# Two blocks side by side at the joints, and token-half sums out of PSUM

## The chip, the cores and the metric

The kernel runs on one core of one Trainium2 chip. The metric is device microseconds of a whole execution; before the change the median of three runs is 968.72 us (968.68 to 970.75). Engine names are those of the profile: PE is TensorE, PEld its weight loads, DVE is VectorE, ACT is ScalarE, POOL is GpSimd, and SP issues the large loads.

## The reference

One layer of a streaming encoder, with 512 tokens and 1024 features, all in float32:

```python
h = h + 0.5 * _swiglu(_rmsnorm(h, ffn1_norm[i]), ffn1_w_in[i], ffn1_w_out[i])
z = _rmsnorm(h, mix_norm[i]) @ w_in[i]
...
h = h + jnp.concatenate([y_conv, y_gla], axis=-1) @ w_out[i]
h = h + 0.5 * _swiglu(_rmsnorm(h, ffn2_norm[i]), ffn2_w_in[i], ffn2_w_out[i])
gate = jax.nn.sigmoid(_rmsnorm(h, ple_norm[i]) @ ple_w_gate[i])
h = h + gate * (p[i] @ ple_w_proj[i])
return _rmsnorm(h, final_norm)
```

What matters here is that four times a new norm of h feeds a projection. The norm's row factor is applied after the projection, so the projection itself takes h times the gain vector, transposed so that features lie on partitions.

## The kernel before, in words

Every float32 product is made of three fast matmuls. Each operand x is split into a high part H (x rounded to the fast format, a copy by ACT) and a low part L (x − H, by DVE), and a product is wH·xH, wH·xL and wL·xH, added up in PSUM (`mm3`, line 209). The program has seven PSUM banks for such sums (`bank`, line 96) and one more for small things (`aux`).

A **joint** is the place where one stage has finished h and the next one needs it transposed. There are three: from FFN1 to the mixer (around 365 us in the trace), from the mixer to FFN2 (around 546 us) and from FFN2 to the last stage, the embedding gate (around 895 us). `Turn` (line 427) does it: `half(e)` takes four of the eight feature chunks; `chunk(c)` transposes chunk c of the four token blocks into one bank by four PE transposes, splits it by `gsplit` (H on ACT, hgH in the trace; L on DVE, hgL; both read the bank and multiply by the gain), and, if the next stage wants it, calls `keep`. `half(0)` runs before the last piece of h is finished, `half(1)` after it. `rows` makes the row factors from the sums of squares, through DVE, a power on POOL and DVE again, and `spread` turns them by four transposes on PE.

`keep` (line 321) is for the two stages that multiply by a Strassen-like scheme with seven products of half size: FFN2 and the last stage (FFN1 keeps its own way and isn't touched). They need sums and differences of the token halves of h (tokens 0 to 255 and 256 to 511) and of its feature halves. `keep` makes two raw copies of a chunk, one per token half, by ACT from PSUM to SBUF, each 128 x 256 (xg in the trace). For FFN2 the sums follow from these raw copies: `sums1` (one subtraction of 128 x 512 per pair of chunks, on the early features) and `sums2` (three). `steps` lists the four calls with `operands`, and they are hung between the matmul blocks. The last stage has `row_sums` (line 1477), which adds two raw copies and subtracts the result from a third, and later `row_diff` and `row_last`.

At the joint itself TensorE runs two blocks over the eight chunks. In the mixer they are pb0 and pa0 (`zblock`, lines 938 to 955), in FFN2 g0 and u0 (`plain_block`, lines 1426 to 1434). First both blocks take the four early chunks, then `half(1)` transposes the four late ones, and then one block takes its late chunks and after it the other.

The order of work on PE, DVE and ACT is written by hand up to line 1658: `Ordered` chains each instruction behind the one before it on its engine as in the program text. From `in_order(False)` on, where the last stage's first product `times(x_, a11, b11, first=True)` and its `half(1)` stand, the planner chooses the order, within the data's dependences. POOL's and SP's order is the planner's throughout, nearly. Two engines that read one bank take turns: in the trace `keep`'s copies wait for hgL of the same chunk.

Of the kernel before, what the change touches and what calls it, by code (L numbers as in the profile page):

```python
# [15 lines left out]
P = 128  # L16
# [46 lines left out]
def block_kernel(ctx: ExitStack, tc: tile.TileContext, a: dict, out: bass.AP):  # L63
# [23 lines left out]
    def bt(dt=F32, s="a"):  # L87
        return big.tile([P, SEQ], dt, tag="A", bufs=NA, name=nm(s))
# [7 lines left out]
    def bank():  # L96
        return pp.tile([P, SEQ], F32, tag="mm", bufs=7, name=nm("ps"))
# [36 lines left out]
    def vec(name, c):  # L134
        return vcols[name, c]
# [27 lines left out]
    def gsplit(src, g, s):  # L163
        hi = bt(F32R, s + "H")
        act.activation(hi, src, AF.Copy, scale=g)
        lo = bt(F32R, s + "L")
        dve.scalar_tensor_tensor(out=lo, in0=src, scalar=g, in1=hi.bitcast(F32),
                                 op0=ALU.mult, op1=ALU.subtract)
        return hi, lo
# [63 lines left out]
    def zblock(w, x, mid={}, ps=None, ks=range(DC)):  # L233

        ps = ps if ps is not None else bank()
        for k in ks:
            if k in mid:
                mid[k]()
            wh, wl = rows_of(w, k)
            mm3(ps, wh, wl, *x[k], k == 0, k == DC - 1)  # L240
        return ps
# [57 lines left out]
    def two(t):  # L299
        return t.rearrange("p (k c) -> p k c", k=2)  # L300

    def sub(out, x, y):
        dve.tensor_tensor(out=out, in0=x, in1=y, op=ALU.subtract)
# [3 lines left out]
    class Right:  # L307
# [13 lines left out]
        def keep(self, ps, c, by_dve=False):  # L321

            k, jp, jj = c // 4, c % 4 // 2, c % 2
            for half in range(2):
# [5 lines left out]
                else:  # L330
                    act.activation(o, src, AF.Copy, scale=g)

        def sums1(self, jp):
            b11, b12 = self.raw[0, 0, jp], self.raw[0, 1, jp]
            sub(b11, b12, b11)
# [91 lines left out]
    class Turn:  # L427
# [6 lines left out]
        def done(self, t, e):  # L434
            act.activation(tmp("sq", bufs=3), h_of(t, e), AF.Square, accum_out=self.ss[:, e * TB + t:e * TB + t + 1])

        def chunk(self, c):
            ps = bank()
            for t in range(TB):
                pe.transpose(ps[:, t * P:(t + 1) * P], hall[:, t, c * P:(c + 1) * P], ident)  # L440
            self.hg.append(gsplit(ps, vec(self.gname, c), "hg"))
            if self.x is not None:
                self.x.keep(ps, c)

        def half(self, e):
            for c in range(4 * e, 4 * e + 4):
                self.chunk(c)

        def rows(self):
            ss = tmp("cs", 16)[:, :TB]  # L450
# [484 lines left out]
    low(w2b[1])  # L935
    w2a = [high(raw_a[0])]
    mid = []
    pb0 = zblock(wb[0], hg, ks=range(4))
    pa0 = zblock(wa[0], hg, ks=range(4))
    nxt.half(1)  # L940
    zblock(wb[0], hg, ps=pb0, ks=range(4, DC))
    gw = bt(s="gw")[:, 0:2 * DC * RANK].rearrange("p (k c) -> p k c", k=DC)
    pool.memset(gw, 0.0)
    nc.sync.dma_start(out=gw[:, :, 0:RANK], in_=w_in[:, C_G:C_G + RANK].rearrange("(k p) c -> p k c", p=P))
    w2a.append(high(raw_a[1]))
    raw_q = pair(C_Q)
    low(w2a[0])
    zblock(wa[0], hg, {4: lambda: mid.append(nxt.rows())}, pa0, range(4, DC))
    low(w2a[1])
    pb1 = zblock(wb[1], hg, {1: lambda: mid.append(spread(mid[0]))})  # L950
    rs, rsb = mid
# [472 lines left out]
        return ps  # L1424

    mid = []
    steps = xb.steps()
    g0 = plain_block(w0, 0, 0, ks=range(4))
    u0 = plain_block(w0, 1, 0, ks=range(4))
    nxt.half(1)  # L1430
    steps[0]()
    plain_block(w0, 0, 0, ps=g0, ks=range(4, DC))
    steps[1]()
    plain_block(w0, 1, 0, ps=u0, ks=range(4, DC))
    w1.fetch("a21", "a22")
    w1.add_part("a11", "a12")
    g1_ = plain_block(w0, 0, 1, {3: lambda: mid.append(nxt.rows()), 7: lambda: mid.append(spread(mid[0]))})
# [1 line left out]
    w2.fetch("a11", "a21", "a22", "a12")  # L1439
    w1.add_part("a21", "a22")  # L1440
    u1_ = plain_block(w0, 1, 1)
    steps[2]()
    steps[3]()
    hooks = sums_hooks(xb, ("t2", "t3", "t1", "t4"), (("h0", 1), ("h1", 1), ("h3", 1), ("m1", 2)))
    hooks.update({("h2", 1): lambda *_: w2.s12(), ("h4", 1): lambda *_: w2.s3_(), ("m7", 10): lambda *_: turn_p(0), ("m5", 10): lambda *_: turn_p(1)})

# [27 lines left out]

    HS = [slice(h * HALF, (h + 1) * HALF) for h in range(2)]

    def row_sums(jp):

        a11_, a21_, a22_ = (xp.raw[k, h, jp] for k, h in ((0, 0), (0, 1), (1, 1)))
        s1.append(a22_)  # L1480
        dve.tensor_tensor(out=a22_, in0=a21_, in1=a22_, op=ALU.add)
        n2.append(two(bt(s="n2")))
        sub(n2[jp], a11_, a22_)

    def q_high(to, src, jp):
        to.append(added(high(src[jp])))
# [24 lines left out]
                  ("d20", 1): todo((q_high, b21, q21, 1), (first_sum, 1), (third_sum, 1)),  # L1511
                  ("d20", 2): todo((final_in,))})
    hg = []
    xp = Right(hg, "ple_norm")
    nxt = Turn("ple_norm", xp)
    nxt.hg = hg
    rs2_ = mid
# [260 lines left out]
```

## Time and profile before

| | us |
|---|---|
| median of 3 runs | 968.72 |
| the profiled execution | 969.31 |
| its span | 967.5 |
| PE busy in the span | 948.2 |
| DVE busy | 722.5 |
| ACT busy | 476.5 |
| POOL busy | 56.2 |

The span reaches from the first to the last instruction; the execution's own time has 1.8 us around it. Numbers ahead of a row of the order of time are the start in us from the span's beginning, then the row's length; "x4" merges four neighbours alike, and the bracket at the end tells how long the engine had been idle and what ended that. A row of the stages gives for each engine its busy time and, in brackets, its instructions, and behind POOL the clock granted to TensorE as a share of full speed.

### The profile page before, as it was taken

How to read it: one execution, taken by the hardware profiler on the slowest of the kernel's cores; microseconds unless marked ns; L12 is line 12 of the kernel's file. 1: busy time of each engine (PE TensorE's matmuls, PEld its weight loads, DVE VectorE, ACT ScalarE, POOL GpSimd, SP SyncE). 2: the span in 40 equal slices, each digit the busy share in tenths (PEclk: the TensorE clock that was granted, in tenths of full speed). 3: DMA queues.
4: the chain of work that ended last, by engine and by line, in shares of the span. 5: the costliest groups of instructions: out<-in, count | busy, mean ns of one | idle time of the engine just before them, and what ended most of it. 6: DMA issues, size and time to landing. Idle time of an engine off the chain costs nothing.

```text
span 967.5 us, 14435 instructions
## 1 busy us (share of the span) xinstructions
PE 948.2 (98%) x5810; PEld 833.0 (86%) x5810; DVE 722.5 (75%) x967; ACT 476.5 (49%) x733; POOL 56.2 (6%) x71
## 2 busy tenths in 40 slices
PE   9999999999999999999999999999999999999895
PEld 7888999999999987788878689999999999998574
DVE  6775877877777567999985367777777768766796
ACT  5552444434443464473656564344433444345983
POOL 0000200000000111001210010000000000001121
PEclk9999999999999999999999999999999999999998
DMA  7541333243233594253563371432233322455452
GB/s 226 176 152 44 97 103 107 67 130 110 91 103 112 153 221 92 63 142 97 146 159 101 75 174 44 131 110 88 92 106 112 120 95 66 153 196 131 87 98 98
DMA packets 90214, 112.88 MB, mean 117 GB/s; under 512 B 5075, under 2 KB 65669, under 8 KB 90148
## 3 DMA queue, kind: packets, MB, share of 16 engines
q1 hardware_dynamic: 84260, 94.67, 31.1%
q0 software_dynamic: 5872, 17.30, 9.8%
q8 instruction: 45, 0.74, 0.3%
q14 instruction: 21, 0.17, 0.1%
q10 hardware_dynamic: 16, 0.00, 0.0%
HBM read 93.61 MB, written 2.10 MB: 99 GB/s over the span
## 4 chain that ended last, share of the span: by engine, by line
PE 93%; ACT 3%; DVE 2%; issue 0%; DMA 0%; POOL 0%; POOLq 0%; SPq 0%; ACTq 0%; DVEq 0%
PE ps L46 92%; ACT xg L46 1%; PE ax L46 1%; ACT hgH L46 1%; ACT wh L46 1%; ACT sq L46 1%; DMA wr<-in_ffn_w_in 0%; DVE hgL L46 0%; DVE g L46 0%; DVE s L46 0%; ACT wl L46 0%; DVE rs L46 0%; DVE y L46 0%; DVE sq L46 0%; DVE xg L46 0%
## 5 line engine op out<-in xcount | busy, mean ns | idle before, releaser
L46 PE MATMUL ps<-hgH,wh 128*128 128x256 f32 (+1 forms) x768 | 239.7, 317 | 2.2 <-ACT hgH L46 1.7
L46 PE MATMUL ps<-hgL,wh 128*128 128x256 f32 (+1 forms) x768 | 239.1, 316 | 0.3 <-DVE hgL L46 0.3
L46 PE MATMUL ps<-hgH,wl 128*128 128x256 f32 (+1 forms) x768 | 238.2, 315 | 0.0
L46 DVE TENSOR_TENSOR wl<-wr,wh 128x1024 fp32r<-128x1024 f32 (+1 forms) x158 | 188.6, 1208 | 61.0 <-ACT wh L46 60.8
L46 ACT CAST wh<-wr 128x1024 fp32r<-128x1024 f32 (+1 forms) x172 | 176.3, 1039 | 74.3 <-PE ps L46 41.4
L46 PEld LDWEIGHTS ps<-hgH,wh 128*128 128x128 f32 x768 | 146.9, 191 | 14.7 <-ACT hgH L46 4.3
L46 PEld LDWEIGHTS ps<-hgL,wh 128*128 128x128 f32 x768 | 146.6, 191 | 11.2 <-DVE hgL L46 1.9
L46 PEld LDWEIGHTS ps<-hgH,wl 128*128 128x128 f32 x768 | 147.0, 191 | 8.7
L46 PE MATMUL ps<-wh,actH 128*128 128x512 f32 x352 | 137.6, 391 | 0.0
L46 PE MATMUL ps<-wh,actL 128*128 128x512 f32 x352 | 137.3, 390 | 0.0
L46 PE MATMUL ps<-wl,actH 128*128 128x512 f32 x352 | 137.0, 389 | 0.0
L46 ACT ACTIVATE s<-g 128x512 f32<-128x512 f32 x48 | 30.4, 632 | 156.3 <-DVE g L46 156.3
L46 DVE SCALAR_TENSOR_TENSOR hall<-ps,rsh,hall 128x512 f32<-128x512 f32 x96 | 71.1, 747 | 30.1 <-PE ps L46 29.2
L46 DVE SCALAR_TENSOR_TENSOR cv<-glu,cw,cv 128x502 f32<-128x502 f32 (+24 forms) x120 | 81.0, 730 | 0.6
L46 PEld LDWEIGHTS ps<-wl,actH 128*128 128x128 f32 x352 | 66.1, 188 | 13.9
L46 PEld LDWEIGHTS ps<-wh,actH 128*128 128x128 f32 x352 | 66.2, 188 | 12.9
L46 PEld LDWEIGHTS ps<-wh,actL 128*128 128x128 f32 x352 | 66.2, 188 | 12.4
L46 ACT CAST wh<-sm 128x1024 fp32r<-128x1024 f32 x38 | 39.7, 1046 | 42.0 <-DVE sm L46 36.2
L46 DVE TENSOR_TENSOR wl<-sm,wh 128x1024 fp32r<-128x1024 f32 x38 | 46.3, 1220 | 4.6 <-ACT wh L46 4.3
L46 ACT COPY sq<-ps 128x512 f32<-128x512 f32 x38 | 22.1, 585 | 54.8 <-PE ps L46 54.8
L46 DVE SCALAR_TENSOR_TENSOR hgL<-ps,vcol,hgH 128x512 fp32r<-128x512 f32 x32 | 23.2, 748 | 30.9 <-ACT hgH L46 30.7
L46 DVE TENSOR_TENSOR sm<-wr,wr 128x1024 f32<-128x1024 f32 x17 | 21.0, 1236 | 29.5 <-DMA wr<-in_ffn_w_in 29.5
(247 smaller groups left out, 1691.7 us busy)
## 6 DMA issues: line engine op xcount, KB each, us to landing
wr<-in_ffn_w_in SPq DMA_DIRECT2D x84, 512.0 KB
wr<-in_ffn_w_out SPq DMA_DIRECT2D x44, 512.0 KB
wr<-in_w_in SPq DMA_DIRECT2D x20, 512.0 KB
wl<-wr POOLq DMA_DIRECT2D x15, 512.0 KB, 5.3
wr<-in_w_out SPq DMA_DIRECT2D x8, 512.0 KB
wq<-in_ple_w_gate SPq DMA_DIRECT2D x8, 512.0 KB
wl<-wq POOLq DMA_DIRECT2D x8, 512.0 KB, 4.6
wa<-wr POOLq DMA_DIRECT2D x12, 256.0 KB, 6.1
```

Source lines behind the costliest of these rows:

```text
L46: inst = call(*args, **kwargs)
```

## The change

It has three parts.

**The loop over k.** In the mixer and in FFN2 the two blocks at the joint run chunk by chunk: for each k first the one block's three matmuls, then the other's. `half(1)` stands ahead of k = 4, in the mixer `rows` ahead of k = 6 (it stood at the second block's fourth chunk, behind the memset and load of gw and one weight remainder).

**The four chunks first.** `half` makes all four chunks' transposes and splits, and only then whatever `turned` of the next stage gave back for each chunk.

**The sums from PSUM.** For FFN2 the early chunks (c under 4) are still copied raw, now after the splits, with `sums1` behind each pair. The late chunks are not copied at all: `sums` makes the three differences of a chunk by three multiply-subtracts on DVE, each 128 x 256, which read the bank and multiply by the gain. `steps` isn't called any more. For the last stage the class `Rows` copies one token half of a late chunk by ACT and adds the other from PSUM by DVE; `row_sums` has only its subtraction left.

```diff
--- before.py
+++ after.py
@@ -330,6 +330,21 @@
                 else:
                     act.activation(o, src, AF.Copy, scale=g)
 
+        def turned(self, ps, c):
+            if c < 4:
+                return lambda: (self.keep(ps, c), self.sums1(c // 2) if c % 2 else None)
+            return lambda: self.sums(ps, c)
+
+        def sums(self, ps, c):
+            jp, jj, g = c % 4 // 2, c % 2, vec(self.gname, c)
+            b21, b22 = ps[:, 0:HALF], ps[:, HALF:SEQ]
+            if not jj:
+                for half in (1, 0):
+                    self.raw[1, half, jp] = two(bt(s="xg"))
+            t1, t3, t2, t4 = (self.raw[i, half, jp][:, jj] for i, half in ((0, 0), (0, 1), (1, 1), (1, 0)))
+            for out_, b, x in ((t3, b22, t3), (t2, b22, t1), (t4, b21, t2)):
+                dve.scalar_tensor_tensor(out=out_, in0=b, scalar=g, in1=x, op0=ALU.mult, op1=ALU.subtract)
+
         def sums1(self, jp):
             b11, b12 = self.raw[0, 0, jp], self.raw[0, 1, jp]
             sub(b11, b12, b11)
@@ -434,17 +449,17 @@
         def done(self, t, e):
             act.activation(tmp("sq", bufs=3), h_of(t, e), AF.Square, accum_out=self.ss[:, e * TB + t:e * TB + t + 1])
 
-        def chunk(self, c):
-            ps = bank()
-            for t in range(TB):
-                pe.transpose(ps[:, t * P:(t + 1) * P], hall[:, t, c * P:(c + 1) * P], ident)
-            self.hg.append(gsplit(ps, vec(self.gname, c), "hg"))
-            if self.x is not None:
-                self.x.keep(ps, c)
-
         def half(self, e):
+            late = []
             for c in range(4 * e, 4 * e + 4):
-                self.chunk(c)
+                ps = bank()
+                for t in range(TB):
+                    pe.transpose(ps[:, t * P:(t + 1) * P], hall[:, t, c * P:(c + 1) * P], ident)
+                self.hg.append(gsplit(ps, vec(self.gname, c), "hg"))
+                if self.x is not None:
+                    late.append(self.x.turned(ps, c))
+            for f in late:
+                f()
 
         def rows(self):
             ss = tmp("cs", 16)[:, :TB]
@@ -935,17 +950,20 @@
     low(w2b[1])
     w2a = [high(raw_a[0])]
     mid = []
-    pb0 = zblock(wb[0], hg, ks=range(4))
-    pa0 = zblock(wa[0], hg, ks=range(4))
-    nxt.half(1)
-    zblock(wb[0], hg, ps=pb0, ks=range(4, DC))
+    pb0, pa0 = bank(), bank()
+    for k in range(DC):
+        if k == 4:
+            nxt.half(1)
+        if k == 6:
+            mid.append(nxt.rows())
+        zblock(wb[0], hg, ps=pb0, ks=(k,))
+        zblock(wa[0], hg, ps=pa0, ks=(k,))
     gw = bt(s="gw")[:, 0:2 * DC * RANK].rearrange("p (k c) -> p k c", k=DC)
     pool.memset(gw, 0.0)
     nc.sync.dma_start(out=gw[:, :, 0:RANK], in_=w_in[:, C_G:C_G + RANK].rearrange("(k p) c -> p k c", p=P))
     w2a.append(high(raw_a[1]))
     raw_q = pair(C_Q)
     low(w2a[0])
-    zblock(wa[0], hg, {4: lambda: mid.append(nxt.rows())}, pa0, range(4, DC))
     low(w2a[1])
     pb1 = zblock(wb[1], hg, {1: lambda: mid.append(spread(mid[0]))})
     rs, rsb = mid
@@ -1424,14 +1442,13 @@
         return ps
 
     mid = []
-    steps = xb.steps()
-    g0 = plain_block(w0, 0, 0, ks=range(4))
-    u0 = plain_block(w0, 1, 0, ks=range(4))
-    nxt.half(1)
-    steps[0]()
-    plain_block(w0, 0, 0, ps=g0, ks=range(4, DC))
-    steps[1]()
-    plain_block(w0, 1, 0, ps=u0, ks=range(4, DC))
+    g0, u0 = bank(), bank()
+    for k in range(DC):
+        if k == 4:
+            nxt.half(1)
+            xb.operands()
+        plain_block(w0, 0, 0, ps=g0, ks=(k,))
+        plain_block(w0, 1, 0, ps=u0, ks=(k,))
     w1.fetch("a21", "a22")
     w1.add_part("a11", "a12")
     g1_ = plain_block(w0, 0, 1, {3: lambda: mid.append(nxt.rows()), 7: lambda: mid.append(spread(mid[0]))})
@@ -1439,8 +1456,6 @@
     w2.fetch("a11", "a21", "a22", "a12")
     w1.add_part("a21", "a22")
     u1_ = plain_block(w0, 1, 1)
-    steps[2]()
-    steps[3]()
     hooks = sums_hooks(xb, ("t2", "t3", "t1", "t4"), (("h0", 1), ("h1", 1), ("h3", 1), ("m1", 2)))
     hooks.update({("h2", 1): lambda *_: w2.s12(), ("h4", 1): lambda *_: w2.s3_(), ("m7", 10): lambda *_: turn_p(0), ("m5", 10): lambda *_: turn_p(1)})
 
@@ -1474,13 +1489,25 @@
 
     HS = [slice(h * HALF, (h + 1) * HALF) for h in range(2)]
 
+    class Rows(Right):
+
+
+        def turned(self, ps, c):
+            if c < 4:
+                return lambda: self.keep(ps, c)
+            jp, jj, g = c % 4 // 2, c % 2, vec(self.gname, c)
+            if not jj:
+                self.raw[1, 0, jp] = two(bt(s="xg"))
+                s1.append(two(bt(s="s1")))
+            act.activation(self.raw[1, 0, jp][:, jj], ps[:, 0:HALF], AF.Copy, scale=g)
+            dve.scalar_tensor_tensor(out=s1[jp][:, jj], in0=ps[:, HALF:SEQ], scalar=g, in1=self.raw[0, 1, jp][:, jj],
+                                     op0=ALU.mult, op1=ALU.add)
+            return lambda: None
+
     def row_sums(jp):
 
-        a11_, a21_, a22_ = (xp.raw[k, h, jp] for k, h in ((0, 0), (0, 1), (1, 1)))
-        s1.append(a22_)
-        dve.tensor_tensor(out=a22_, in0=a21_, in1=a22_, op=ALU.add)
         n2.append(two(bt(s="n2")))
-        sub(n2[jp], a11_, a22_)
+        sub(n2[jp], xp.raw[0, 0, jp], s1[jp])
 
     def q_high(to, src, jp):
         to.append(added(high(src[jp])))
@@ -1511,7 +1538,7 @@
                   ("d20", 1): todo((q_high, b21, q21, 1), (first_sum, 1), (third_sum, 1)),
                   ("d20", 2): todo((final_in,))})
     hg = []
-    xp = Right(hg, "ple_norm")
+    xp = Rows(hg, "ple_norm")
     nxt = Turn("ple_norm", xp)
     nxt.hg = hg
     rs2_ = mid
```

## The prediction

> **What bounds the kernel now.** I read the page first (busy time, the chain that ended last), then busy time by stage, then the order of time at each of the three joints.
>
> ```profile
> span 967.5 us, 14435 instructions
> PE 948.2 (98%) x5810; PEld 833.0 (86%) x5810; DVE 722.5 (75%) x967; ACT 476.5 (49%) x733; POOL 56.2 (6%) x71
> ...
> PE 93%; ACT 3%; DVE 2%; issue 0%; DMA 0%; POOL 0%; POOLq 0%; SPq 0%; ACTq 0%; DVEq 0%
> ```
>
> TensorE sets the end for 93% of the span; 7% belongs to others. The stages around the joints show where that lies, apart from the kernel's start and tail:
>
> ```profile
> core 0: us, PE busy (x) PEld busy (x) DVE busy (x) ACT busy (x) POOL busy (x), PEclk, DMA share, GB/s
> 364.00:374.00 10.00, 9.98 (x54) 8.22 (x53) 5.97 (x13) 3.56 (x6) 1.05 (x1) 1.00 0.19 52
> 546.00:560.00 14.00, 12.04 (x42) 7.80 (x41) 5.92 (x10) 9.55 (x16) 1.92 (x3) 0.76 0.05 10
> 555.00:558.00 3.00, 3.00 (x7) 2.40 (x8) 2.79 (x6) 3.00 (x5) 0.00 (x0) 0.50 0.00 0
> 897.00:907.00 10.00, 8.91 (x37) 5.45 (x37) 7.30 (x10) 8.36 (x18) 0.00 (x0) 1.00 0.64 120
> 907.00:922.00 15.00, 11.87 (x49) 7.83 (x48) 11.31 (x21) 14.67 (x27) 4.37 (x5) 1.00 0.34 65
> ```
>
> The mixer's joint (364 on) has no hole. The FFN2 joint (546 on) loses TensorE time and clock: 0.76 granted, 0.50 in its middle. In the last joint (897 to 922) ACT is nearly full, 14.67 of 15, while TensorE has holes: ACT is the bound there.
>
> **FFN2 joint, the loop over k.** This is the order of time in it:
>
> ```profile
> 546.05 1.91 PE L46 MATMUL ps<-ident,hall 128*128 128x128 f32 x16
> 546.69 0.69 ACT L46 ACTIVATE hgH<-ps,vcol 128x512 fp32r<-128x512 f32 x1 [4.13 <-PE ps L46]
> 547.41 0.75 DVE L46 SCALAR_TENSOR_TENSOR hgL<-ps,vcol,hgH 128x512 fp32r<-128x512 f32 x1 [5.75 <-ACT hgH L46]
> 548.20 0.84 ACT L46 ACTIVATE xg<-ps,vcol 128x256 f32<-128x256 f32 x2 [0.82 <-DVE hgL L46]
> 548.22 0.50 PE L46 MATMUL ps<-hgL,wh 128*128 128x512 f32 x1
> 548.93 0.69 ACT L46 ACTIVATE hgH<-ps,vcol 128x512 fp32r<-128x512 f32 x1
> 549.67 0.50 PE L46 MATMUL ps<-hgH,wh 128*128 128x512 f32 x1 [0.72 <-ACT hgH L46]
> 551.90 0.80 PE L46 MATMUL ps<-hgH,wh 128*128 128x512 f32 x1 [0.71 <-ACT hgH L46]
> ...
> 558.89 0.39 PE L46 MATMUL ps<-hgH,wl 128*128 128x512 f32 x1
> 559.80 0.39 PE L46 MATMUL ps<-hgH,wh 128*128 128x512 f32 x1
> ```
>
> ACT works in written order: hgH of a chunk, then that chunk's two raw copies xg, which wait 0.82 for hgL. So a chunk comes every 549.67 to 551.90 = 2.23 us, while one block eats it in three matmuls of (559.80 − 558.89)/4 = 0.2275, or 0.68 us. Behind the waits the matmuls run at half rate: 7 in the 3 us of the stage shown above, 0.43 each. Of the 24 matmuls of g0's and u0's later halves the second starts at 548.22, and the next block starts at 559.80.
>
> After the change no raw copy stands between the splits, so they come as in the mixer's joint, which has none:
>
> ```profile
> 365.57 2.42 ACT L46 ACTIVATE hgH<-ps,vcol 128x512 fp32r<-128x512 f32 x4 [3.33 <-PE ps L46]
> 366.30 2.73 DVE L46 SCALAR_TENSOR_TENSOR hgL<-ps,vcol,hgH 128x512 fp32r<-128x512 f32 x4 [4.87 <-ACT hgH L46]
> 367.10 0.19 PEld L46 LDWEIGHTS ps<-hgL,wa 128*128 128x128 f32 x1 [0.33 <-DVE hgL L46]
> 367.44 0.63 PE L46 MATMUL ps<-hgH,wa 128*128 128x512 f32 x2
> ```
>
> Four hgH in 2.42 and four hgL in 2.73: a chunk every 0.66 us, hgL of the four ready at about 548.2, 548.8, 549.5 and 550.1. Two blocks side by side eat a chunk in six matmuls, 1.37 us, so only the first chunk is waited for. The second matmul stays at 548.22, the third follows 0.34 later (367.10 to 367.44), the next block starts 22 × 0.2275 after that: 548.22 + 0.34 + 5.0 = 553.57 in place of 559.80. **Gain 6.2 us**, provided the clock stays full, as it did in the mixer's joint.
>
> **FFN2 joint, what replaces the copies.** ACT loses 8 copies of c4 to c7; DVE loses the 6 subtractions of 512 after them and gains 12 multiply-subtracts of 256 out of PSUM. No row shows exactly that one. The nearest:
>
> ```profile
> L46 DVE TENSOR_SCALAR xg<-ps,vcol 128x256 f32<-128x256 f32 x8 | 3.5, 474 | 0.0
> ...
> 596.90 1.43 DVE L46 TENSOR_TENSOR hgL<-xg,hgH 128x256 fp32r<-128x256 f32 x4 [1.11 <-ACT hgH L46]
> ```
>
> At least 1.43/4 = 0.36 (no PSUM), at most the 0.75 of a 512-wide hgL; I take 0.43, between the 0.36 and the 474 ns of the PSUM-fed 256-wide row, as durations overlap in a queue. Twelve are 5.2 us, from 550.1 to 555.3 (554.4 to 559.1 at the bounds). Their readers are splits written behind later blocks, but the row sums for the norm queue right behind them on DVE:
>
> ```profile
> 557.57 0.16 DVE L46 TENSOR_TENSOR cs<-ssq 128x4 f32<-128x4 f32 x1
> ...
> 560.62 0.16 DVE L46 TENSOR_TENSOR rs<-rs,rs 128x4 f32<-128x4 f32 x1
> ...
> 564.56 0.60 PE L46 MATMUL ax<-ident,rs 128*128 128x128 f32 x4
> ```
>
> The chain cs to rs took 560.78 − 557.57 = 3.2 us here: 555.3 + 3.2 = 558.5. TensorE wants rs 21 matmuls into the next block: 553.57 + 4.8 = 558.35. That is 0.2 us late; I count nothing, since POOL's part of the chain comes behind two DMA issues for w1's sums, which ACT now feeds right behind the splits, some 5 us earlier. At the upper bound it is 3.9 us late, and the gain falls to 2.3.
>
> A rule speaks against this edit. The Trainium skill, "VectorE: DVE Perf Modes", section "Rules for kernel authors", says to accept the slow PSUM source or to copy to SBUF first where many operations follow; its errata section gives VectorE 120 + elements cycles at 0.96 GHz out of PSUM, an estimate of 0.39 us each, 4.7 us for twelve. By it the rows above would be done 0.5 us earlier than by mine; the sum stays.
>
> **Earlier half of this joint.** The copies of c0 to c3 move behind all four splits; the two subtractions of sums1 move up behind them and so ahead of the last additions to h on DVE.
>
> ```profile
> 532.30 0.67 ACT L46 ACTIVATE hgH<-ps,vcol 128x512 fp32r<-128x512 f32 x1
> ...
> 540.38 1.28 DVE L46 TENSOR_TENSOR hall<-ps,hall 128x512 f32<-128x512 f32 x2
> ```
>
> 532.30 + 2.42 + four pairs of copies at 0.73 (548.20 to 548.93) = 537.6, and 0.7 more for sums1: 538.3, ahead of the 540.38 at which these additions ran; the four banks are free 8 us before the transposes of 546.05 want them. Cost 0. If that cover went, each us past 546 would be one on the path.
>
> **Mixer's joint.** Interleaving removes nothing: the one wait is the 0.33 at its head, and it stays. The row sums overtake one weight remainder of 1.22 us on DVE; the SP load that waits for that buffer starts some 2.3 us later. Its use lies behind a sigmoid on ACT:
>
> ```profile
> 368.94 1.22 DVE L46 TENSOR_TENSOR wl<-wr,wh 128x1024 fp32r<-128x1024 f32 x1
> 376.23 1.03 ACT L46 CAST wh<-wr 128x1024 fp32r<-128x1024 f32 x1
> ```
>
> Freed at 370.2, cast at 376.23: 6 us for a load, 3.7 after. If that doesn't do, ACT slips 1 or 2 us and with it the gate of the next GLU block, whose PSUM bank is not wanted at once. On POOL the power of the norm is now written ahead of the memset of gw, and SP's load of gw behind that:
>
> ```profile
> 370.52 1.05 POOL L46 TENSOR_TENSOR rs<-ms,negh 128x4 f32<-128x4 f32 x1 [26.04 <-DVE ms L46]
> ```
>
> POOL's order isn't written by hand, and POOL sat idle for 26.04 us ahead of the power, the memset long done. If it stays behind the power now, gw is loaded after 371.6, and SP's next load waits for its issue; gw is read three blocks of 24 matmuls, 5.5 us each, after the joint. Gain 0; bounds −0.5 (the slip reaches TensorE) and +0.3 (the head's wait goes).
>
> **Last joint.** Here the order is left to the planner from the later half on.
>
> ```profile
> 896.86 0.67 ACT L46 ACTIVATE hgH<-ps,vcol 128x512 fp32r<-128x512 f32 x1
> 902.93 0.84 ACT L46 ACTIVATE xg<-ps,vcol 128x256 f32<-128x256 f32 x2 [0.82 <-DVE hgL L46]
> 905.04 1.40 DVE L46 SCALAR_TENSOR_TENSOR hall<-ps,rsh,hall 128x512 f32<-128x512 f32 x2
> 905.16 0.84 ACT L46 ACTIVATE xg<-ps,vcol 128x256 f32<-128x256 f32 x2 [0.82 <-DVE hgL L46]
> 907.17 0.67 ACT L46 ACTIVATE hgH<-ps,vcol 128x512 fp32r<-128x512 f32 x1
> 919.97 0.62 ACT L46 CAST sH<-n 128x512 fp32r<-128x512 f32 x1 [0.33 <-DVE n L46]
> 921.19 0.49 PE L46 MATMUL ps<-wh,sL 128*128 128x512 f32 x1 [0.76 <-DVE sL L46]
> ```
>
> The early copies go behind four splits: these end at 896.86 + 2.42, so the last additions to h no longer wait on DVE until 905.04 for the fourth hgL. In the later half four copies leave ACT (4 × 0.36 to 0.42, 1.5 us); DVE trades two additions of 512 (0.7 each, as the two in the row of 905.04) for four of 256 from PSUM (0.43), +0.3 us. ACT's waits for hgL (0.82 twice, and 0.33 before the last cast of the sum) go too. ACT being the bound, **gain 1.5 + 2.0 = 3.5 us** at 921.19, from where TensorE is dense again. Bounds: 0, if other work of ACT takes the freed place ahead of the splits; above, all of TensorE's holes: 86 instructions, 16 of them transposes of 0.12, are 70 × 0.2275 + 1.9 = 17.8 of the 25 us, so 7.1.
>
> **Sum:** 969.31 (the profiled execution: span 967.5 and 1.8 around it) − 6.2 − 0 − 3.5 = 959.6. The median of the runs is 968.72, 0.6 lower; I say 959.0.
>
> **Rivals.**
> - *Last joint stays ACT-bound:* the planner fills the freed time with casts due later. ACT at 14.67 of 15 speaks for it; that four copies are really gone, against. 968.7 − 6.2 = 962.5.
> - *Last joint becomes TensorE-bound:* all holes close. For it: the early hgL no longer paced by copies; against: DVE, 11.31 of 15 busy, must do the same work in less. 968.7 − 6.2 − 7.1 = 955.4.
> - *The sums hold the norm up:* DVE at 0.75 per sum, 3.9 us of new wait on TensorE, whose order there is written. Against: 474 ns. 968.7 − 2.3 − 3.5 = 962.9.
> - *The clock falls anyway.* At half rate for the some 6.2 us from 551.9 to past 558 a dense TensorE loses 3.1: 962.1. For: no wait ahead of the fall was longer than 0.72, and the last joint's waits let none follow. The Trainium skill, "TensorE: Matmul & The Clock Gate", section "What's actually happening", halves the clock after an idle window of about 3.4 us; by that rule these waits weren't its cause. The trace disagrees: 0.50 without such a window.
> - *Slower:* in the last joint the late copies hold four of seven banks. If the planner puts ACT's other work of 897 to 922 (8.36 + 14.67, less 8 splits of 0.6 and 16 copies of 0.42: 11.5 us) ahead of them, the later transposes and hgH slip from 907.17. It decides from 6.2 us of slip on, hgH after 913.4; at 7 us the time is 969.5. Against: the early half is still in written order, copies ready first.
>
> **How the numbers follow.** Forecast 0.62; ACT-bound 0.16; TensorE-bound 0.10; sums 0.05; clock 0.04; slower 0.03. The range takes ACT-bound, sums and clock in at its top and most of the TensorE-bound case below: 955.8 to 963.0. A change within 0.2% (1.9 us) can't be told from none: faster 0.95, same 0.02, slower 0.03.
>
> **What would show it.** Right: hgH of the FFN2 joint as one row x4, the next block 5.4 us after the second matmul that follows the transposes, clock 1.00 there, no wait of the norm's transposes; the last cast before the dense stretch (now 919.97) 3 to 4 us closer to the first hgH (now 896.86). Wrong: waits on DVE for the norm, clock below 1.00 after 548, hgH c4 of the last joint no earlier, or new holes of TensorE after 922.

## The result, and the profile after

The changed kernel takes 960.34 us (median of 4 runs, 959.98 to 960.76), the kernel before 968.70 beside it (968.43 to 970.75): a ratio of 0.9909, 95% interval 0.9892 to 0.9927. The profiled execution took 960.76 us. Its page first, the same lines as before: span, busy time, and the share of each engine in the chain that ended last.

```profile
span 959.0 us, 14433 instructions
PE 943.4 (98%) x5810; PEld 832.5 (87%) x5810; DVE 723.6 (75%) x975; ACT 472.1 (49%) x721; POOL 55.9 (6%) x71
...
PE 95%; ACT 2%; DVE 1%; DMA 0%; issue 0%; POOL 0%; POOLq 0%; SPq 0%; ACTq 0%; DVEq 0%
```

ACT has 12 instructions fewer and DVE 8 more, and TensorE sets the end for 95% of the span (93 before). Where the time went is seen by stage, in the changed kernel's busy times (columns as in the prediction):

```profile
546.00:560.00 14.00, 13.98 (x73) 11.58 (x71) 8.87 (x23) 6.71 (x10) 2.76 (x3) 1.00 0.48 97
555.00:558.00 3.00, 3.00 (x15) 2.48 (x14) 1.61 (x8) 0.00 (x0) 1.03 (x1) 1.00 1.06 197
891.00:901.00 10.00, 8.56 (x40) 5.76 (x39) 8.14 (x13) 9.88 (x24) 0.30 (x1) 1.00 0.67 126
901.00:914.50 13.50, 10.95 (x47) 7.59 (x45) 10.56 (x21) 11.63 (x18) 5.27 (x5) 1.00 0.52 92
```

The FFN2 joint is full: 73 matmuls in 14 us where 42 ran before, at a clock of 1.00 in place of 0.76. The last joint (the two lower rows) still has holes of 1.44 and 2.55 us, in 23.5 us. The order of time of the changed kernel at the first two joints (first fence; "..." stands for rows left out), and three rows of the kernel before (second fence), show how much of the 8.55 us between the two profiled executions belongs to the FFN2 joint:

```profile
355.62 1.91 PE L46 MATMUL ps<-ident,hall 128*128 128x128 f32 x16
...
546.60 1.91 PE L46 MATMUL ps<-ident,hall 128*128 128x128 f32 x16
547.24 2.42 ACT L46 ACTIVATE hgH<-ps,vcol 128x512 fp32r<-128x512 f32 x4 [4.38 <-PE ps L46]
547.97 2.73 DVE L46 SCALAR_TENSOR_TENSOR hgL<-ps,vcol,hgH 128x512 fp32r<-128x512 f32 x4 [5.92 <-ACT hgH L46]
...
548.77 0.50 PE L46 MATMUL ps<-hgL,wh 128*128 128x512 f32 x1
...
550.61 5.30 DVE L46 SCALAR_TENSOR_TENSOR xg<-ps,vcol,xg 128x256 f32<-128x256 f32 x12
...
554.10 0.39 PE L46 MATMUL ps<-hgH,wh 128*128 128x512 f32 x1
...
558.00 0.16 DVE L46 TENSOR_TENSOR rs<-rs,rs 128x4 f32<-128x4 f32 x1
...
558.86 0.60 PE L46 MATMUL ax<-ident,rs 128*128 128x128 f32 x4
...
886.86 1.91 PE L46 MATMUL ps<-ident,hall 128*128 128x128 f32 x16
```

```profile
355.01 1.91 PE L46 MATMUL ps<-ident,hall 128*128 128x128 f32 x16
...
892.55 1.91 PE L46 MATMUL ps<-ident,hall 128*128 128x128 f32 x16
...
919.00 0.64 ACT L46 CAST sH<-n 128x512 fp32r<-128x512 f32 x1
```

Read distances, not places, for the two executions are shifted against each other by their starts: 355.62 against 355.01 stands ahead of everything that the change touches. From there to the later half's transposes at the FFN2 joint it is 190.98 us (before 546.05 − 355.01 = 191.04): the mixer's joint brought 0.06. From those transposes to the first ones of the last joint it is 886.86 − 546.60 = 340.26 (before 346.50): the FFN2 joint brought **6.24**. The last joint, changed kernel:

```profile
891.17 0.67 ACT L46 ACTIVATE hgH<-ps,vcol 128x512 fp32r<-128x512 f32 x1
...
896.85 1.40 DVE L46 SCALAR_TENSOR_TENSOR hall<-ps,rsh,hall 128x512 f32<-128x512 f32 x2
...
900.28 0.69 ACT L46 ACTIVATE hgH<-ps,vcol 128x512 fp32r<-128x512 f32 x1
...
904.19 0.47 PE L46 MATMUL ps<-wh,hgH 128*128 128x512 f32 x1 [1.65 <-DVE s L46]
...
908.58 0.68 ACT L46 ACTIVATE hgH<-ps,vcol 128x512 fp32r<-128x512 f32 x1
...
910.08 0.48 ACT L46 ACTIVATE xg<-ps,vcol 128x256 f32<-128x256 f32 x1 [0.82 <-DVE hgL L46]
...
911.46 1.05 ACT L46 CAST wh<-wq 128x1024 fp32r<-128x1024 f32 x1 [0.91 <-PE ps L46]
...
912.42 1.13 ACT L46 CAST sH<-n 128x512 fp32r<-128x512 f32 x2
...
913.86 0.50 PE L46 MATMUL ps<-wh,sL 128*128 128x512 f32 x1
```

From the first hgH to the first sL, where TensorE becomes dense, it is 913.86 − 891.17 = 22.69 us (before 921.19 − 896.86 = 24.33): the last joint brought **1.64**. Behind it nothing changed up to the last DVE instruction (41.28 us in both). The sum closes: + 0.55 at the start (546.60 − 546.05), − 6.24, − 1.64, and − 1.17 between the last DVE instruction and the end of the span, where only the output's stores are left, make − 8.50, as the spans have it. The 1.17 can't be put down to one part of the change: that stretch takes 4.28 us in the kernel before and 4.32 in the same kernel with its waits filled, but 3.07 to 3.56 in the first four experiments below, each of which has a part of the old form, and 3.11 in the changed kernel. Why it is longer in those two is not shown.

### The profile page after: what moved, and what is told of

Its sections match the earlier page's. It is cut to its first block, busy times and chain, and to the rows that moved or that the text cites. A ratio compares the mean times of both kernels' runs of the same rounds, so it can differ in the third digit from the quotient of the medians.

```text
span 959.0 us, 14433 instructions
## 1 busy us (share of the span) xinstructions
PE 943.4 (98%) x5810; PEld 832.5 (87%) x5810; DVE 723.6 (75%) x975; ACT 472.1 (49%) x721; POOL 55.9 (6%) x71
## 4 chain that ended last, share of the span: by engine, by line
PE 95%; ACT 2%; DVE 1%; DMA 0%; issue 0%; POOL 0%; POOLq 0%; SPq 0%; ACTq 0%; DVEq 0%
PE ps L46 94%; PE ax L46 1%; ACT wh L46 1%; DMA wr<-in_ffn_w_in 0%; ACT sq L46 0%; DVE s L46 0%; DVE g L46 0%; ACT hgH L46 0%; DVE rs L46 0%; DVE y L46 0%; ACT wl L46 0%; DVE wl L46 0%; POOL rs L46 0%; ACT wq L46 0%; POOLq L1801 0%
## 5 line engine op out<-in xcount | busy, mean ns | idle before, releaser
L46 ACT CAST actH<-m 128x512 fp32r<-128x512 f32 x44 | 25.6, 619 | 31.9 <-DVE m L46 31.9
```

The costliest lines, as they stand in the source:

```text
L46: inst = call(*args, **kwargs)
```

## The experiments

Two distances are read from every trace as above: **A**, from the later half's transposes at the FFN2 joint to the first transposes of the last joint, and **B**, from the first hgH of the last joint to the first sL. They are free of the start's shift. Ratios are to the runs of the kernel before on the same chip.

| kernel | A | B | median us | ratio, 95% interval |
|---|---|---|---|---|
| before | 346.50 | 24.33 | 968.70 | |
| changed | 340.26 | 22.69 | 960.34 | 0.9909, 0.9892 to 0.9927 |
| FFN2 joint alone | 340.30 | 24.33 | 961.68 | 0.9908, 0.9893 to 0.9923 |
| last joint alone | 347.17 | 23.88 | 968.38 | 0.9971, 0.9961 to 0.9981 |
| splits first alone | 340.28 | 24.33 | 964.02 | 0.9929, 0.9912 to 0.9946 |
| loop over k alone | 342.90 | 24.33 | 966.64 | 0.9956, 0.9941 to 0.9971 |
| changed, sums in SBUF | 340.31 | 22.67 | 962.03 | 0.9893, 0.9877 to 0.9910 |
| changed, sums twice | 347.39 | 22.68 | 967.82 (one run) | |
| changed, eighth bank | 340.27 | 22.47 | 961.14 | 0.9894, 0.9878 to 0.9910 |
| changed, split written later | 340.54 | 22.67 | 960.79 | 0.9887, 0.9872 to 0.9902 |
| before, waits filled | 344.92 | 24.32 | 968.67 | 0.9986, 0.9974 to 0.9997 |
| order by hand, eight banks | 340.30 | 18.92 | 959.23 | 0.9891, 0.9875 to 0.9908 |
| order by hand, seven banks | 340.31 | 19.32 | 957.79 | 0.9878, 0.9863 to 0.9893 |
| changed, late copies | 340.27 | 21.68 | 959.22 | 0.9888, 0.9871 to 0.9905 |

The kernel before had medians of 971.60 beside the first four experiments, 971.86 beside the next four (sums in SBUF to split written later), 970.15 beside the filled waits and the two orders by hand, and 970.46 beside the last; its times reach from 968.4 to 972.5. Several of the kernels differ by less than that, so A and B decide. They come from one profiled execution of each.

**FFN2 joint alone.** `Right.turned`, `Right.sums` and the loop over k, as in the change; the last joint and the mixer's loop as before:

```diff
-    xp = Rows(hg, "ple_norm")
+    xp = Plain(hg, "ple_norm")
+    class Plain(Right):
+        def turned(self, ps, c):
+            self.keep(ps, c)
+            return lambda: None
```

> Before, with the change made at the FFN2 joint alone (splits first, loop over k, sums from PSUM); the mixer's and the last joint are as before. If the prediction's step for this joint holds and the mixer's joint brings nothing, the time falls by 6.2 us, to 962.5, the granted clock in the 14 us from the later half's transposes is 1.00 (0.76 before), and the first transposes of the last joint come 6.2 us earlier. If the mixer's joint carries part of the gain, less than 6.2 is seen here.

A is 340.30, 6.20 less, and from the mixer's transposes to this joint's it is 545.96 − 354.93 = 191.03, as before. The granted clock of its 14 us from the transposes on is 1.00. The whole gain of this part lies here, and the mixer's loop carries none.

**Last joint alone.** `Rows` and `row_sums` as in the change, the FFN2 joint as before.

> Before, with the change made at the last joint alone. By the prediction's step (four copies gone and three waits of ACT gone) 3.5 us: 965.2, and the first sL before the dense stretch comes 3.5 us nearer to the first hgH of this joint (24.33 us before). By what the trace of the whole change shows there, 1.6 us up to the dense stretch (22.69 us); then 967.1, and a TensorE wait of over 1 us on a bank that DVE's sum from PSUM still reads. If something of the end gains too, up to 2.8 us: 965.9.

B is 23.88, a gain of 0.45 only, and the median of 968.38 is above every forecast. TensorE waits 1.65 us on a bank here, too. The busy times of this run show what else held it up (the last three columns are the granted clock, the DMA share and GB/s):

```profile
910.00:912.00 2.00, 1.52 (x5) 1.32 (x6) 1.16 (x3) 2.00 (x4) 0.18 (x1) 0.80 0.00 0
912.00:914.00 2.00, 2.00 (x6) 1.54 (x6) 1.75 (x3) 0.83 (x2) 0.68 (x1) 0.50 0.47 92
```

The clock fell to 0.50 in the middle of the joint in this execution, six matmuls in 2 us where ten run at 1.00. (A is 0.67 longer than before. At the FFN2 joint the fall came and went later, with 0.70 from 552 to 554, before 0.50, and 0.59 from 558 to 560, before 0.92; so more of it lay behind the last split, where TensorE doesn't wait.) In the profiled executions of before and of the changed kernel it didn't; in those of splits first and loop alone, which have the old form there, it fell around the first sL (914 to 920 and 916 to 922), and from there to the last DVE instruction it took 1.45 and 1.56 us more than the 41.28 of the kernel before; in the one with the waits filled 1.61 more. So a measured time can hold a chance term of some 1.5 us at this joint, in its old form and in the new one.

**Splits first alone.** The raw copies go behind the four splits; blocks in turn and sums in SBUF, as before:

```diff
+        def turned(self, ps, c):
+            return lambda: self.keep(ps, c)
```

> Before, with one thing changed at the FFN2 joint: the four splits of each half come first and the raw copies behind them. The two blocks follow each other as before, the sums stay in SBUF and at their old places, no sum from PSUM. My theory: the gain is the order of the splits, since one block takes a chunk in 0.68 us and the splits come every 0.66 us: 6.2 us, 962.5, clock 1.00 at this joint. Rival, the prediction's words (the loop over k makes the gain): with the blocks in turn each chunk is waited for, and no more than 3 us are gained: 965.7 or above.

The order of time at the FFN2 joint of this run, and the last joint's first transposes:

```profile
546.04 1.91 PE L46 MATMUL ps<-ident,hall 128*128 128x128 f32 x16
546.68 2.42 ACT L46 ACTIVATE hgH<-ps,vcol 128x512 fp32r<-128x512 f32 x4 [4.38 <-PE ps L46]
...
553.56 0.39 PE L46 MATMUL ps<-hgH,wh 128*128 128x512 f32 x1
...
886.32 1.91 PE L46 MATMUL ps<-ident,hall 128*128 128x128 f32 x16
```

The next block starts 553.56 − 546.04 = 7.52 us after the transposes (before 13.75, changed 7.50). The order of the splits is the whole gain: A falls by 6.22, with neither the loop over k nor a sum from PSUM. The splits come every 0.66 us and one block takes a chunk in 0.68, so it never waits for the second one to share. The median of 964.02 is 1.5 above what was expected. The clock at the last joint, as said, fits that: three of the four executions have a mean clock of 0.995 and took 963.73 to 964.74 us, the fourth has 0.997 and took 962.53.

**Loop over k alone.** Blocks side by side, each chunk's raw copies ahead of the next split as before.

> Before, with the two blocks of the FFN2 joint side by side, and the chunks in the old order: each chunk's raw copies stand ahead of the next split. A chunk every 2.23 us, and six matmuls of 0.2275 = 1.37 us for each. My theory: the last chunk's hgL is ready some 7.4 us after the first (555.6), then six matmuls: the next block at 557.0 in place of 559.80, a gain of 2.8 us at full clock (965.9), and 1.4 less if the matmuls behind the waits run at half rate again. Rival, the loop makes the gain: 6.2 us, 962.5. On the clock: if waits of some 0.9 us between short bursts bring it down, it shows under 1.00 here again; if not, 1.00.

```profile
545.82 1.91 PE L46 MATMUL ps<-ident,hall 128*128 128x128 f32 x16
...
552.44 0.84 ACT L46 ACTIVATE xg<-ps,vcol 128x256 f32<-128x256 f32 x2 [0.82 <-DVE hgL L46]
...
555.96 0.39 PE L46 MATMUL ps<-hgH,wh 128*128 128x512 f32 x1
```

```profile
552.00:554.00 2.00, 1.69 (x7) 0.95 (x6) 0.51 (x2) 1.42 (x3) 0.00 (x0) 1.00 0.00 0
```

The first fence is the order of time, the second the busy times of the same run. The copies still wait 0.82 and the chunks still come every 2.23 us, yet A falls by 3.60, not 2.8: the last hgL came earlier than I worked out, and the clock stayed at 1.00, with seven matmuls in the 2 us in which before had three at 0.50. So each of the two alone gives something, but together they give no more than the order of the splits does: they work on the same waits.

**Sums in SBUF.** The changed kernel, with the twelve sums of this joint made from late raw copies:

```diff
-            return lambda: self.sums(ps, c)
+            return lambda: (self.keep(ps, c), self.sums2(c % 4 // 2) if c % 2 else None)
```

> The changed kernel, with the sums of the FFN2 joint's later half taken as before: the four splits, then raw copies on ACT, then six subtractions of 512 in SBUF, at the place of the twelve from PSUM. My theory: at this joint the sums from PSUM are not what gains, since the copies lie behind the splits on ACT and nothing on TensorE waits for them. From the later half's transposes to the first transposes of the last joint 340.3 us, as in the changed kernel (340.26; before 346.50), and 960.3 in all. Rival: with eight copies of 0.37 more on ACT and DVE waiting for them, the row sums for the norm come late: rs later than 558.9 by 1 to 3 us, and the time by as much.

```profile
552.75 4.20 DVE L46 TENSOR_TENSOR xg<-xg,xg 128x512 f32<-128x512 f32 x6 [0.46 <-ACT xg L46]
```

A is 340.31: the same. Six subtractions in SBUF took 4.20 us after a wait of 0.46 for the copies, twelve from PSUM 5.30. With this run's transposes at 548.20 the six end 8.75 us after them and the twelve (555.91 − 546.60) 9.31. The sums from PSUM spare ACT eight copies, and at this joint that is worth nothing.

**Sums twice.** Each of the twelve sums from PSUM is preceded by one that is thrown away:

```diff
+            for x in (t3, t1, t3):
+                dve.scalar_tensor_tensor(out=t4, in0=b22, scalar=g, in1=x, op0=ALU.mult, op1=ALU.subtract)
```

> The changed kernel, with each of the twelve sums from PSUM of the FFN2 joint preceded by one more that is thrown away: 12 x 0.44 = 5.3 us more of DVE work between the splits and the row sums for the norm. The trace of the changed kernel leaves the norm some 0.7 us of slack (rs done 558.16, its transposes at 558.86 without a wait). So TensorE should wait 5.3 - 0.7 = 4.6 us on DVE ahead of these transposes, and the time be 964.9 to 965.4. Rival: the planner or the order moves the row sums ahead, or the slack is larger, and the time rises by less than 2 us.

```profile
550.55 11.53 DVE L46 SCALAR_TENSOR_TENSOR xg<-ps,vcol,xg 128x256 f32<-128x256 f32 x24
...
564.39 1.11 PE L46 MATMUL ax<-ident,rs 128*128 128x128 f32 x4 [5.36 <-DVE rs L46]
```

```profile
564.00:566.00 2.00, 1.61 (x6) 1.51 (x7) 0.47 (x3) 0.46 (x1) 0.00 (x0) 0.54 0.04 8
```

Twelve more took 11.53 − 5.30 = 6.23 us (0.52 each, more than the 5.3 expected), and TensorE waited 5.36: the slack of the norm's chain was 0.87. The cover is real and thin. The time rose by more than the wait: behind it the clock was 0.54 (second fence), and A is 7.13 longer.

**Waits filled.** The kernel before, with matmul work that is thrown away in TensorE's waits:

```diff
-    plain_block(w0, 0, 0, ps=g0, ks=range(4, DC))
+    plain_block(w0, 0, 0, {5: fill, 6: fill, 7: fill}, g0, range(4, DC))
+    def fill(n=8):
+        ps = aux()
+        for _ in range(n):
+            pe.transpose(ps[:, 0:P], ident, ident)
```

> Before, with eight transposes of the identity into the auxiliary bank (0.1 us each, thrown away) ahead of each of the chunks c5 to c7 in g0's later half at the FFN2 joint, where TensorE waits some 1.5 us per chunk. My theory: the clock of 0.50 there comes from TensorE having too little work over several us (three matmuls per 2.23 us before; six per 2.23 us, in the kernel with the loop alone, kept 1.00), so with the filling it stays at 1.00, and the 14 matmuls behind the last split run in 3.2 in place of 4.4 us: 1.0 to 1.4 us less from the transposes to the last joint (345.1 to 345.5 in place of 346.50 and 347.17). Rival: the fall has nothing to do with the waits and comes anyway: 0.50 again and no gain.

The first fence is the kernel before, the second the filled one:

```profile
548.00:550.00 2.00, 1.27 (x4) 0.48 (x3) 0.52 (x2) 1.42 (x3) 0.00 (x0) 1.00 0.00 0
550.00:552.00 2.00, 1.00 (x4) 0.40 (x3) 0.52 (x2) 1.41 (x3) 0.00 (x0) 0.88 0.01 4
552.00:554.00 2.00, 1.91 (x3) 0.69 (x3) 0.64 (x1) 1.33 (x3) 0.00 (x0) 0.50 0.00 0
```

```profile
552.00:554.00 2.00, 1.72 (x11) 1.23 (x10) 0.54 (x1) 1.42 (x3) 0.00 (x0) 1.00 0.00 0
```

The clock stayed at 1.00 and A fell by 1.58, though the chunks came no faster. The times of all executions agree, with a ratio of 0.9986, or 1.4 us. Of the 6.24 us some 1.6 are therefore the clock, and the remaining 4.7 the waits themselves; that split is an estimate, for the fall cost 0.67 more in another execution of the same FFN2 joint (last joint alone).

**Eighth bank.** `x_, y_ = [bank(), bank()], [bank(), aux()]` at the last joint of the changed kernel.

> The changed kernel, with the second bank of y_ in the last joint taken from the auxiliary bank, which lies idle there: eight banks in place of seven. My theory: the 1.65 us that TensorE waits at 904.19 is a bank held by the sum from PSUM on DVE. With the eighth bank that wait goes, and the first hgH to the first sL takes 21.0 to 22.0 us (22.69 in the changed kernel; 24.33 before): 958.7 to 959.7. Rival: ACT is the bound, the wait only moves to the next split, and 22.6 or more remain: 960.3.

```profile
903.65 0.47 PE L46 MATMUL ps<-wh,pTH 128*128 128x512 f32 x1 [0.94 <-DVE s L46]
...
912.18 0.73 PE L46 MATMUL ps<-wh,sH 128*128 128x512 f32 x2 [1.42 <-ACT sH L46]
```

The rival is the nearer: B falls by 0.22, to 22.47. The 1.65 us on the bank shrank to 0.94 and moved to the inputs' product, and TensorE's wait for the cast sH grew from 0.75 to 1.42. The bank was a wait, but ACT's cast of the row sums sets the end.

**Split written later.** Half of the third product's weight splits is written behind the second product in the program text.

> The changed kernel, with the second of the two negated weight splits for the third product of the last joint (a cast and a scaled copy of 1.05 each on ACT, and a summing DMA) written behind the matmuls of the second product in place of ahead of the row sums. My theory: ACT bounds the joint through other work between its splits, so 2.1 us less of it ahead of the last split bring the first sL some 1.5 to 2.1 us nearer to the first hgH (20.6 to 21.2 us in place of 22.69): 958.2 to 958.8. Rival: TensorE's bank or DVE binds instead and less than 0.5 is gained; or the late summing DMA is waited for by the third product, and what is gained is given back there.

B is 22.67: nothing. Both pairs of cast and scaled copy for the third product still stand ahead of hgH c7 (908.38), at 902.45 and 903.97 and at 906.11 and 907.07. Place in the text isn't place in the queue where the planner chooses, so this run doesn't test ACT's order; the next two do.

**Order by hand, eight and seven banks.** Copies and sums behind the four splits, the weight casts tied behind the copies or behind the cast of the row sums, and the norm's row sums behind the sums from PSUM:

```diff
+            def later():
...
+            return later
     nxt.half(1)
+    copied, taken = act.latest, dve.latest
...
-        act.behind(act.latest, squared)
+        act.behind(act.latest, copied)
...
     n2_ = [x for jp in range(2) for x in split_rows(n2, jp)]
+    cast = act.latest
...
     times(x_, n2_, b2)
+    b3 = []
+    for t in t3:
+        w = high(t)
+        act.behind(act.latest, cast)
+        b3.append(added(w))
+        act.behind(act.latest, cast)
```

> The changed kernel, with an order for the last joint written by hand: the copies and sums from PSUM of the later half behind all four splits, the casts of the second, third and fifth products' weights behind those or behind the cast of the row sums, the row sums for the norm behind the sums from PSUM, and the eighth bank as in the run with the auxiliary bank. My theory: ACT's order is the bound (8.3 us from the first to the fourth split of the later half, where 2.4 do; then a weight cast ahead of the row sums' cast). With it free, TensorE's own work remains: 24 matmuls of the second product and 12 of the inputs from 901.3 on, 8.4 us: the first sL at 910 to 910.8 of the changed kernel's clock, 18.8 to 19.6 us after the first hgH (22.69), and 956.4 to 957.3 in all. Rivals: the weights of the third product come too late by the moved casts, and TensorE waits for them behind the dense start, by up to 2 us; or the sums wait on DVE and nothing is gained.

> The kernel with the order written by hand, but with seven banks as in the changed kernel: the second bank of y_ is again one that a later half's chunk leaves behind. My theory: the copies and sums now stand behind all four splits, so that bank comes free some 2 us after them (about 904.5 to 905) and TensorE waits there up to 3 us; of the gain by order 1 to 2 us remain: the first sL 20.5 to 22 us after the first hgH. Rival: banks do not matter beside ACT's order: as with eight banks within 0.3.

Of the order with seven banks:

```profile
890.51 0.67 ACT L46 ACTIVATE hgH<-ps,vcol 128x512 fp32r<-128x512 f32 x1
...
899.61 0.69 ACT L46 ACTIVATE hgH<-ps,vcol 128x512 fp32r<-128x512 f32 x1
...
905.66 1.23 ACT L46 CAST sH<-n 128x512 fp32r<-128x512 f32 x2 [0.75 <-DVE n L46]
...
909.83 0.39 PE L46 MATMUL ps<-wh,sL 128*128 128x512 f32 x1
```

With eight banks B is 18.92, as expected; the time of 959.23 is not the 956.4 to 957.3 that was, for this execution started 1.21 us later than that of the changed kernel (first transposes at 356.83) and gave back 0.98 at the end. With seven it is 19.32, 0.40 more, so the rival of that run is near and my 20.5 to 22 far: banks matter little beside ACT's order. From hgH c4 to the first cast of the row sums ACT now takes 905.66 − 899.61 = 6.05 us, in place of 912.42 − 900.28 = 12.14, and from 899 to the first sL TensorE has no more wait that the profile lists. Some is given back: from the first sL to the last DVE instruction it is 42.02 us with seven banks and 42.26 with eight, in place of 41.28. With eight banks the third product waits for its late weights:

```profile
920.26 0.50 PE L46 MATMUL ps<-wl,sH 128*128 128x512 f32 x1 [0.36 <-DMA wl<-wq]
```

**The order by hand with seven banks beats both kernels**: 957.79 us (957.44 to 958.56), 2.55 below the changed kernel's median, and no run of the one reaches into the other's. They did not run side by side, but the distances inside the traces agree: from the first hgH to the last DVE instruction it is 61.34 us with seven banks and 61.18 with eight, 63.97 in the changed kernel. These kernels move the copies and sums, the weight casts and the norm's row sums at once; the next run takes the first of these alone.

**Late copies alone.** One thing changed in `Rows.turned`: the copy and the sum are returned and run behind the splits.

```diff
-            return lambda: None
+            return later
```

> The changed kernel with one thing changed: at the last joint the copy and the sum from PSUM of the chunks c4 to c7 are written behind the four splits, as at the FFN2 joint; all else is left to the planner, which still puts a weight cast or scaled copy behind the second, third and fourth split. Theory: in the changed kernel each copy between two splits shares its bank with hgL and the sum, and ACT's queue waits there. Summed from the durations, ACT runs from the first split of the later half to the first cast of the row sums in 8.1 us in place of 12.1, so TensorE's own work binds again: first sL 19.0 to 20.5 us after the first hgH (22.69 in the changed kernel, 19.32 in the order by hand with seven banks), 957.5 to 958.6 in all. Rival: the casts between the splits are what held the last split up, and they remain: 22 us or more, 960.

```profile
904.56 0.50 PE L46 MATMUL ps<-wh,hgL 128*128 128x512 f32 x1 [0.83 <-DVE hgL L46]
```

```profile
905.52 1.59 ACT L46 ACTIVATE xg<-ps,vcol 128x256 f32<-128x256 f32 x4
...
909.07 0.61 ACT L46 CAST sH<-n 128x512 fp32r<-128x512 f32 x1
```

Both a little: the cast of the row sums comes 9.17 us after hgH c4 (899.90), against 12.14 and 6.05, and B is 21.68, a third of the way. Of the 3.12 us that are left to the order by hand, 2.85 are there when the late copies start: 905.52 − 899.90 = 5.62 us behind hgH c4, by hand 902.38 − 899.61 = 2.77. In between the planner puts two weight casts and a scaled copy, 0.95 us each (TensorE waits 0.83 at the third chunk). That the casts are what is left follows from these rows; no run moves them alone.

## Why the prediction was right, and where not

**The sum.** 959.6 was forecast for a profiled execution that took 960.76, and 959.0 for a median of 960.34. The terms: − 6.2 for − 6.24; − 3.5 for − 1.64; 0 for − 0.06; and − 0.6 of starts and stores that no term had. That last one is luck: by the other three as measured the profiled execution would have taken 961.4, 1.8 above the forecast, and the 0.6 hides a third of that.

**FFN2 joint, the loop over k.** Size and picture right: hgH x4 in 2.42 and hgL x4 in 2.73, the next block 554.10 − 548.77 = 5.33 us after the second matmul behind the transposes (forecast 5.35), clock 1.00. What stands behind it was half right. The step stood under the loop over k. It rested on both, the raw copies gone from between the splits and two blocks side by side that eat a chunk in 1.37 us; the run with the splits first shows the same 6.22 with the blocks in turn, since 0.66 and 0.68 us match as well. The loop is a second remedy for the same wait (3.60 alone) and adds nothing to the first.

**What replaces the copies.** Right: 0.44 per sum (forecast 0.43), 5.30 in all (5.2). The norm, which I had 0.2 us late and counted at nothing, was 0.87 early, as the doubled sums show. The rival of the sums holding up the norm has its mechanism shown there, 5.36 us of wait for 6.23 of extra work; its price of 0.75 per sum was never near. That the sums from PSUM are no source of gain at this joint was not in the prediction, and the run with sums in SBUF shows it.

**Earlier half and mixer's joint.** Nothing, as forecast: 0.06 for the mixer's, and no wait of the transposes at 546.60 on the early banks.

**The clock falls anyway.** It didn't at this joint, in any profiled execution with the splits first, nor in the one with the loop alone; where I made a long wait, with the sums twice, it did. The mean clock over the whole span agrees: 0.990 to 0.995 in 41 executions of the kernel before, 0.995 to 0.997 with its waits filled, 0.996 to 0.998 in the changed kernel. The filled waits show what it hung on, and that some 1.6 us of the gain were its.

**Last joint.** This is the step that was mis-sized: 1.64 for 3.5. The prediction added the four copies that leave ACT in the later half (1.5) and ACT's waits for hgL (2.0: twice 0.82, in rows of the earlier half, and 0.33 ahead of the last cast), on the ground that ACT is the bound. The stretches say where each went.

- Earlier half, from hgH c0 to hgH c4: 900.28 − 891.17 = 9.11 us, before 907.17 − 896.86 = 10.31. **1.20 won** of the 1.64: the two waits went, and the additions to h ran 5.68 us behind hgH c0 in place of 8.18; from there to the transposes TensorE is busy without a wait. The four splits took 4.38 us (891.17 to 895.55) and not the 2.42 carried over from the mixer's joint, for three weight casts stand between them, as they did before.
- Later half, from hgH c4 to the first cast of n: 12.14, before 919.00 − 907.17 = 11.83. **0.31 lost**, where 1.5 were to be won.
- From that cast to the first sL: 1.44, before 2.19. **0.75 won**, where 0.33 was forecast.

So the term of the four copies failed. ACT had less to do in the later half, 10.28 us busy in place of 11.83, but the time didn't follow: it now waits 0.82 for hgL (the copy of c7) and 0.91 for TensorE (the next weight cast), where it didn't wait before. The planner put the same four weight casts and two scaled copies ahead of the row sums, two of them now between hgH c4 and c5, so that the fourth split comes 8.30 us behind the first (before 914.84 − 907.17 = 7.67). That is the lower bound of that step, "other work of ACT takes the freed place", and the rival "stays ACT-bound" half come true. The end of the last cast, named as the sign, came 1.35 us closer to the first hgH (22.38 in place of 23.73), not 3 to 4. The runs ordered by hand show that it was what stands ahead on ACT, and not how much ACT does in all: with the same number of ACT instructions as the changed kernel (721), B falls to 18.92, 5.4 below before, where I had put 7.1 as the most.

**TensorE-bound** and **slower** did not come. The bank wait that the slower rival feared was there (1.65 us on a bank that DVE's sum still read), but by the run with an eighth bank it cost 0.2, since ACT's cast came last anyway.

## What to carry to other kernels

Where one engine's queue makes pieces that TensorE eats, write the pieces that it waits for first and everything that merely shares their source behind them; test that order alone before restructuring the consumer, as two remedies for one wait do not add. Count a freed instruction as a gain only where the order is fixed: a planner fills the place, and what counts is the time from the first piece to the instruction that releases TensorE. Compare distances between landmarks inside the trace, since the start and the stores moved by as much here as half of the terms in question.

## What was not expected of the hardware

**TensorE's clock falls without a long wait, and filling prevents it.** In the kernel before no wait in front of the fall was longer than 0.72 us, with TensorE busy for 2.27 us of the 4 from 548 to 552; eight small transposes per wait kept 1.00. Where the limit lies, no run here shows. The Trainium skill, "TensorE: Matmul & The Clock Gate", section "What's actually happening", ties the half rate to an idle window of some 3.4 us; the run with the sums twice fits that (0.54 behind a wait of 5.36), the kernel before does not. The same page's section "A second HAM failure mode: psum-queue depth-cycling" says that frequent small idle spells between groups of matmuls can set it swinging as well. The trace agrees so far that it fell to 0.50 behind waits of at most 0.72; at this joint it shows one fall and one return (0.92 from 558 to 560), no repeated swing.

**The start varies.** The first transposes of the mixer's joint, ahead of all that was changed, stood between 354.81 and 357.24 us. The difference arises in the first 20 us. The same four matmuls, in the run with sums in SBUF (transposes at 357.24) and in the order by hand with seven banks (354.94):

```profile
6.65 2.05 PE L46 MATMUL ps<-hgH,wh 128*128 128x512 f32 x4 [0.41 <-DVE wh L46]
```

```profile
6.35 1.17 PE L46 MATMUL ps<-hgH,wh 128*128 128x512 f32 x4 [0.66 <-DVE wh L46]
```

The one takes 2.05 us, the other 1.17, while the clock column says 1.00 for both (6 to 12 us): there the column doesn't show the rate, and the length of the row does. What slows these matmuls is not shown. The profiled executions of the two orders by hand (959.21 and 957.44) differ by this, 356.83 against 354.94, more than by their banks.
